# Gate and up projection of a SwiGLU layer as seven products of block sums (Strassen's scheme) in place of eight block products

## The chip, the cores and the metric

The kernel runs on 1 core of one Trainium2 chip, as one launch. The metric is the device time of one execution in microseconds (us). TensorE (PE) multiplies matrices into PSUM; VectorE (DVE), ScalarE (ACT) and GpSimd (POOL) work on elements; SyncE (SP) issues most of the DMAs. PEld is TensorE's loading of a stationary operand, which has an instruction of its own (LDWEIGHTS) ahead of each matmul.

## The reference

One residual layer on 512 tokens of width 1024, with 16 meta tokens ahead of them, all in float32: two kinds of attention, gates, an output projection, and then the part that this change is about, a SwiGLU feed-forward of width 2816 (22 blocks of 128):

```python
    merged = gates[:, :, 0] * y_sb + gates[:, :, 1] * y_df
    h = h + merged @ w_out[l]
    hn = rmsnorm(h, norm_ffn_g[l])
    h = h + (jax.nn.silu(hn @ w_ffn_gate[l]) * (hn @ w_ffn_up[l])) @ w_ffn_down[l]
y = rmsnorm(h, norm_final_g)
```

## The kernel before

**Precision.** Every float32 operand of a projection is split in two parts: `split` (L73 to L75) casts it to a rounded format on ScalarE (the high part, L74) and subtracts that on VectorE (the low part, L75). A product is then three matmuls, high by high, high by low and low by high (`mm3`, L142 to L147), which accumulate in one PSUM region. The stationary operand is a 128x128 block, the moving one has up to 512 columns.

**Weights.** All weight tiles stand in one list, `stream`, in the order of use; a tile is 128 partitions by 1024 numbers (512 KB). `stage` issues their DMAs on SP into `wst` (three buffers), up to 5 tiles ahead (STAGE); `weights` splits them into `wh` and `wl` (four buffers each), 2 ahead (READY). Apart from the start of the kernel, whose order is written out by hand, the compiler's planner sets the order on every engine when it compiles, from the order of the program, from priorities (`high_priority(offset=EVAC)` lifts a few instructions) and from its own cost estimates; at run time every engine goes through its list in order.

**Around the change.** `accumulate` (L776) computes `merged @ w_out` in two halves of 512 columns. As each group of 128 tokens is finished, `done` (L842) normalises it into `hn`; `turned(0)` and `turned(1)` (L827) transpose 256 tokens each on TensorE and evacuate them as `hT_h` (ScalarE, L838) and `hT_l` (VectorE, L839), with the 1024 channels on 8 blocks of partitions (`k`) and the tokens along the free axis. Block f = 0 of gate and up (`early`) is computed in two halves of 256 tokens, between the two calls of `turned`.

The loop at L865 then goes over f = 1 to 21. For each f it computes gate (L870) and up (L875): 8 blocks of `k`, three matmuls each, with 512 tokens as moving columns, so 48 matmuls per f. ScalarE applies SiLU (L872), VectorE multiplies (L876), and `split` makes `aT_h` and `aT_l` (L877), which the down projection (`accumulate` with the name "down", L898 and L899) reads as its stationary operand. Of the eight PSUM banks four belong to `ps_mm` (tag `mm`, also used for the transposes) and four to `ps_z` (two tiles of two banks).

Of the kernel before, what the change touches and what calls it, by code (L numbers as in the profile page):

```python
# [16 lines left out]
P = 128  # L17
D = 1024
# [21 lines left out]
def block_kernel(ctx: ExitStack, tc: tile.TileContext, x, meta, norm_mix_g, w_in, w_gate, b_gate,  # L40
# [72 lines left out]
    for half in range(2):  # L113
        for k0 in range(0, NFF, 2):
            rows(("down", half, k0), w_fd, half * 512, k0)

    staged, loaded = [], {}

    def stage(upto):
        for n in range(len(staged), min(len(stream), upto)):  # L120
            _, view, c0, cw, k0, k1 = stream[n]
            st = wpool.tile([P, k1 - k0, cw], F32, tag="wst", bufs=3, name="wst")
            staged.append(st)
            for a, b in ((0, 4), (4, 8)) if n < 2 else ((0, k1 - k0),):
                nc.sync.dma_start(st[:, a:b], view[:, k0 + a:k0 + b, c0:c0 + cw])

    def parts(n):
        k, _, _, cw, k0, k1 = stream[n]
        loaded[k] = tuple(wpool.tile([P, k1 - k0, cw], F32R, tag=t, name=t) for t in ("wh", "wl"))
        return loaded[k]  # L130

    def weights(key):
        at = next(i for i, c in enumerate(stream) if c[0] == key)
        if at < START:
            return loaded[key]
        stage(at + STAGE)
        for n in range(len(loaded), min(len(stream), at + READY)):
            wh, wl = parts(n)
            split(wh, wl, staged[n], nc.gpsimd if n < 3 else None)
        return loaded[key]  # L140

    def mm3(ps, pairs, start=True, stop=True):  # L142
        n = len(pairs)
        for i, (ah, al, bh, bl) in enumerate(pairs):
            nc.tensor.matmul(ps, lhsT=ah, rhs=bh, start=(start and i == 0), stop=False)  # L145
            nc.tensor.matmul(ps, lhsT=ah, rhs=bl, start=False, stop=False)  # L146
            nc.tensor.matmul(ps, lhsT=al, rhs=bh, start=False, stop=(stop and i == n - 1))  # L147

    def proj(ps, w, act, tok, ks=(0, KT)):
        (wh, wl), (ah, al) = w, act  # L150
# [624 lines left out]

    def accumulate(pool, name, act, nk, half, tail, done, banks, pieces=None):  # L776

        ah, al = act
# [7 lines left out]
        def step(k, t, c0, c1):  # L786
            wh, wl = weights((name, half, k // 2 * 2))
            q = slice(t * P, (t + 1) * P)
            mm3((acc[t] if c0 == 0 else extra)[:, c0:c1],
                [(ah[:, k, q], al[:, k, q], wh[:, k % 2, c0:c1], wl[:, k % 2, c0:c1])], k == 0, k == nk - 1)  # L790


        def cuts(t):
            return ((0, 256), (256, 512)) if t == NQ - 1 and pieces else ((0, 512),)

        for k in range(nk - tail):
            for t in range(NQ):
                for c0, c1 in cuts(t):
                    step(k, t, c0, c1)
        for t in range(NQ):  # L800
            for c0, c1 in cuts(t):
                for k in range(nk - tail, nk):
                    step(k, t, c0, c1)
                cs = slice(half * 512 + c0, half * 512 + c1)
                nc.vector.tensor_tensor(hres[:, t, cs], hres[:, t, cs], (acc[t] if c0 == 0 else extra)[:, c0:c1], op=ALU.add)
                sq = pool.tile([P, 512], F32, tag="sq", bufs=1, name="sq")
                s0, s1 = ssq[t][:, 0:1], ssq[t][:, 1:2]
                nc.scalar.activation(sq[:, c0:c1], hres[:, t, cs], AF.Square, accum_out=(s1 if half else s0))
# [11 lines left out]
    with tc.tile_pool(name="outp", bufs=1) as op_:  # L820
        hn = op_.tile([P, NQ, D], F32, name="hn")

        def normed(t):
            r = rstd(ssq[t][:, 1:2], more=ssq[t][:, 0:1])()
            nc.vector.tensor_scalar(hn[:, t], hres[:, t], r, None, op0=ALU.mult)

        def turned(tp):  # L827
            cs = slice(tp * 256, (tp + 1) * 256)
            for k in range(0, KT, 2):
                pt = tr_tile()  # L830
                for i in range(2):
                    for t in range(2):
                        nc.tensor.transpose(pt[:, (2 * i + t) * P:(2 * i + t + 1) * P],  # L833
                                            hn[:, 2 * tp + t, (k + i) * P:(k + i + 1) * P], ident)
                for i in range(2):
                    g = g_ffn[:, k + i:k + i + 1]
                    p = pt[:, i * 256:(i + 1) * 256]
                    nc.scalar.activation(hT_h[:, k + i, cs], p, AF.Copy, scale=g)  # L838
                    nc.vector.scalar_tensor_tensor(hT_l[:, k + i, cs], p, g, hT_h[:, k + i, cs].bitcast(F32),  # L839
                                                   op0=ALU.mult, op1=ALU.subtract)  # L840

        def done(t):  # L842
            normed(t)
            if t == 2:
                turned(0)

        accumulate(op_, "out", (mg_h, mg_l), KT, 0, 0, lambda t: None, "z")
        accumulate(op_, "out", (mg_h, mg_l), KT, 1, 6, done, "mm")

        early = [mm_tile(), mm_tile()]  # L850
        for ps, key in zip(early, (("fg", 0), ("fu", 0))):
            proj(ps[:, 0:256], weights(key), hT, slice(0, 256))
        turned(1)
        for ps, key in zip(early, (("fg", 0), ("fu", 0))):
            proj(ps[:, 256:512], weights(key), hT, slice(256, 512))
        use_table("silu_and_others")
    mid.close()


    with tc.tile_pool(name="ffn", bufs=1) as fp:  # L860
        aT_h = fp.tile([P, NFF, SEQ], F32R, name="aT_h")
        aT_l = fp.tile([P, NFF, SEQ], F32R, name="aT_l")
        gF = fp.tile([P, D], F32, name="gF")
        nc.gpsimd.dma_start(gF, norm_final_g.rearrange("(o d) -> o d", o=1).broadcast_to([P, D]))
        for f in range(NFF):  # L865
            if f == 0:
                pg, pu = early
            else:
                pg = mm_tile()
                proj(pg, weights(("fg", f)), hT, ALL)  # L870
            sg = fp.tile([P, SEQ], F32, tag="sg", bufs=2, name="sg")
            nc.scalar.activation(sg, pg, AF.Silu)  # L872
            if f:
                pu = mm_tile()
                proj(pu, weights(("fu", f)), hT, ALL)  # L875
            nc.vector.tensor_tensor(sg, pu, sg, op=ALU.mult)  # L876
            split(aT_h[:, f], aT_l[:, f], sg)  # L877
# [12 lines left out]

        def gained(t, cs):
            if len(outs) == t:
                outs.append(fp.tile([P, D], F32, tag="outs", name="outs", bufs=2))
# [4 lines left out]
        accumulate(fp, "down", (aT_h, aT_l), NFF, 0, 0, lambda t: None, "z")  # L898
        accumulate(fp, "down", (aT_h, aT_l), NFF, 1, 6, finish, "mm", gained)  # L899


# [27 lines left out]
```

## Time and profile before

| | |
|---|---|
| median of 3 runs | 1004.76 us (1004.44 to 1005.29) |
| profiled execution | 1004.22 us, its span 1002.5 us |
| granted TensorE clock | 0.996 of full speed, mean |
| TensorE matmul busy | 986.8 us, 5529 matmuls |
| weight loads busy | 855.2 us |
| VectorE / ScalarE / GpSimd busy | 526.5 / 451.0 / 109.9 us |
| gate and up, f = 1 to 21 | 645.69 to 874.19 us of the span |
| down projection | from 874.19 us |

The span is what the profile of one execution covers; 1.72 us of that execution's time lie around it. A timeline row gives start, duration, engine, line, operation, destination and source with shapes, and in brackets how long the engine had been idle and what ended that. A row of a group gives total busy time, the mean duration of one, and the idle time before its instructions with what ended it. Matmuls are pipelined: the duration of one is longer than the step from its start to the next one's.

### The profile page before, as it was taken

Reading aid. Unit: us, or ns where it says so; the run is one execution under the profiler, and the core shown is the slowest. Engines: PE = TensorE matmul, PEld = TensorE weight load, DVE = VectorE, ACT = ScalarE, POOL = GpSimd, SP = SyncE. Lnnn points to the kernel's source line nnn. Section 1 sums busy time; section 2 is a strip of 40 time slices with the busy share of each in tenths; the row PEclk is TensorE's granted clock in tenths of the full one; section 3 lists DMA queues with packets and bytes.
Section 4 is the critical chain, followed back from the end, with each engine's and each line's share of the span. In section 5 each row is a group of like instructions: output and inputs, shape, how many; then the busy total and the mean of one; then the engine's idle time right before and its main releaser. Section 6 shows DMA issues by size and latency. Waiting matters only on the chain.

```text
span 1002.5 us, 14077 instructions
## 1 busy us (share of the span) xinstructions
PE 986.8 (98%) x5529; PEld 855.2 (85%) x5529; DVE 526.5 (53%) x974; ACT 451.0 (45%) x848; POOL 109.9 (11%) x152
## 2 busy tenths in 40 slices
PE   7999999999999999999999999999999999999997
PEld 5999899998889999889878888888888888888886
DVE  7665446667777777777763334633333333312323
ACT  5655564555455666555653333623232232311313
POOL 4000000000122121122013220000000000000103
PEclk9999999999999999999999999999999999999998
DMA  6322222222333332333223352433333333232212
GB/s 198 106 64 63 85 85 63 85 64 64 86 105 86 106 85 65 105 85 86 84 84 85 104 177 76 122 91 103 99 91 105 87 103 103 87 105 88 102 42 85
DMA packets 129733, 93.01 MB, mean 93 GB/s; under 512 B 3681, under 2 KB 114434, under 8 KB 129666
## 3 DMA queue, kind: packets, MB, share of 16 engines
q1 hardware_dynamic: 127506, 85.09, 28.2%
q0 software_dynamic: 2000, 6.95, 2.6%
q8 instruction: 43, 0.70, 0.3%
q14 instruction: 24, 0.20, 0.1%
q10 hardware_dynamic: 160, 0.07, 0.0%
HBM read 85.67 MB, written 2.10 MB: 88 GB/s over the span
## 4 chain that ended last, share of the span: by engine, by line
PE 93%; DVE 3%; ACT 2%; issue 0%; DMA 0%; POOL 0%; SPq 0%; DVEq 0%; ACTq 0%; POOLq 0%
PE mm L145 25%; PE mm L146 24%; PE mm L147 24%; PE z L145 4%; PE z L146 4%; PE z L147 4%; PE tr L301 2%; PE z L432 1%; PE z L433 1%; PE tr L276 1%; PE z L325 0%; PE tr L313 0%; DMA xs<-in_x_dram 0%; PE tr L833 0%; DVE xs L608 0%
## 5 line engine op out<-in xcount | busy, mean ns | idle before, releaser
L75 DVE TENSOR_TENSOR wl<-wst,wh 128x1024 fp32r<-128x1024 f32 x150 | 185.8, 1239 | 256.8 <-ACT wh L74 254.3
L74 ACT CAST wh<-wst 128x1024 fp32r<-128x1024 f32 x150 | 157.9, 1052 | 358.7 <-PE mm L146 267.5
L145 PE MATMUL mm<-xT_h,wh 128*128 128x264 f32 (+2 forms) x776 | 249.1, 321 | 1.0 <-DVE dk L413 0.8
L146 PE MATMUL mm<-xT_l,wh 128*128 128x264 f32 (+2 forms) x776 | 246.9, 318 | 0.4 <-DVE xT_l L619 0.3
L147 PE MATMUL mm<-xT_h,wl 128*128 128x264 f32 (+2 forms) x776 | 246.1, 317 | 0.0
L145 PEld LDWEIGHTS mm<-xT_h,wh 128*128 128x128 f32 x776 | 146.1, 188 | 11.7 <-ACT xT_h L618 1.0
L146 PEld LDWEIGHTS mm<-xT_l,wh 128*128 128x128 f32 x776 | 146.0, 188 | 10.1 <-DVE xT_l L619 0.7
L147 PEld LDWEIGHTS mm<-xT_h,wl 128*128 128x128 f32 x776 | 146.0, 188 | 10.0
L146 PE MATMUL mm<-hT_l,wh 128*128 128x512 f32 (+1 forms) x368 | 139.9, 380 | 0.0
L145 PE MATMUL mm<-hT_h,wh 128*128 128x512 f32 (+1 forms) x368 | 139.7, 380 | 0.1
L147 PE MATMUL mm<-hT_h,wl 128*128 128x512 f32 (+1 forms) x368 | 139.7, 380 | 0.0
L145 PEld LDWEIGHTS mm<-hT_h,wh 128*128 128x128 f32 x368 | 69.0, 188 | 13.6 <-ACT hT_h L838 0.4
L146 PEld LDWEIGHTS mm<-hT_l,wh 128*128 128x128 f32 x368 | 69.2, 188 | 13.2 <-DVE hT_l L839 0.2
L147 PEld LDWEIGHTS mm<-hT_h,wl 128*128 128x128 f32 x368 | 69.2, 188 | 13.1
L145 PE MATMUL mm<-o_h,wh 128*128 128x512 f32 x128 | 53.2, 415 | 0.0
L876 DVE TENSOR_TENSOR sg<-mm,sg 128x512 f32<-128x512 f32 x22 | 15.2, 691 | 70.8 <-PE mm L147 70.8
L146 PE MATMUL mm<-o_l,wh 128*128 128x512 f32 x128 | 50.1, 391 | 0.8 <-DVE o_l L504 0.8
L147 PE MATMUL mm<-o_h,wl 128*128 128x512 f32 x128 | 50.1, 391 | 0.0
L282 POOL COPY v_s<-vT 128x16 f32<-128x16 f32 x64 | 21.8, 369 | 210.0 <-ACT vT L287 210.0
L460 ACT ACTIVATE pr<-pr,nm 128x144 f32<-128x144 f32 (+3 forms) x64 | 36.3, 568 | 14.2 <-DVE nm L458 14.1
L145 PE MATMUL z<-wh,aT_h 128*128 128x512 f32 (+1 forms) x110 | 40.5, 368 | 0.0
L146 PE MATMUL z<-wl,aT_h 128*128 128x512 f32 (+1 forms) x110 | 40.5, 368 | 0.0
(227 smaller groups left out, 1538.3 us busy)
## 6 DMA issues: line engine op xcount, KB each, us to landing
wst<-in_w_in_dram SPq DMA_DIRECT2D x46, 512.0 KB, 3.9
wst<-in_w_ffn_gate_dram SPq DMA_DIRECT2D x22, 512.0 KB, 3.8
wst<-in_w_ffn_up_dram SPq DMA_DIRECT2D x22, 512.0 KB, 3.8
wst<-in_w_ffn_down_dram SPq DMA_DIRECT2D x22, 512.0 KB, 3.6
wst<-in_w_gate_dram SPq DMA_DIRECT2D x16, 512.0 KB, 3.9
dk<-dk POOLq DMA_DIRECT2D x16, 264.0 KB, 4.9
wst<-in_w_br_sb_dram SPq DMA_DIRECT2D x8, 512.0 KB, 3.5
wst<-in_w_br_df_dram SPq DMA_DIRECT2D x8, 512.0 KB, 3.6
```

The source lines that it names most:

```text
L74: (hi_copy or nc.scalar.copy)(hi, src)
L75: (lo_eng or nc.vector).tensor_tensor(lo, src, hi.bitcast(F32), op=ALU.subtract)
L145: nc.tensor.matmul(ps, lhsT=ah, rhs=bh, start=(start and i == 0), stop=False)
L146: nc.tensor.matmul(ps, lhsT=ah, rhs=bl, start=False, stop=False)
L147: nc.tensor.matmul(ps, lhsT=al, rhs=bh, start=False, stop=(stop and i == n - 1))
L276: nc.tensor.transpose(pt[:, j * P:(j + 1) * P], vT[:, j * P:(j + 1) * P], ident)
L282: nc.gpsimd.tensor_copy(v_s[:, 32 * t:32 * t + NM], vT[:, (t + 1) * P:(t + 1) * P + NM])
L301: nc.tensor.transpose(pt[:, (t - j) * P:(t - j + 1) * P], blocks(t, j * P, (j + 1) * P), ident)
L432: nc.tensor.matmul(o, lhsT=q[c][:, qs], rhs=k[c][:, 0, k0:k1], start=True, stop=False)
L433: nc.tensor.matmul(o, lhsT=q[c][:, qs], rhs=k[c][:, 1, k0:k1], start=False, stop=True)
L460: nc.scalar.activation(pr[:, c], pr[:, c], AF.Exp, bias=nm[:, c:c + 1], accum_out=ls[:, t, c:c + 1])
L876: nc.vector.tensor_tensor(sg, pu, sg, op=ALU.mult)
```

## The change

For f = 1 to 21, gate and up are taken as a 2x2 matrix of blocks (gate and up, by the two halves K1 and K2 of the 1024 channels), and the activations as another (K1 and K2, by the token halves T1 and T2 of 256). Their product is formed from seven products of block sums (a form of Strassen's scheme with 15 block additions); each of the seven is 4 blocks of `k` by three matmuls of 256 columns, so 84 matmuls of 256 columns per f.

- Activation sums are formed once: ScalarE evacuates each transposed block a second time in full float32 (`bf`), `block_sums` makes the four sums and splits them into `t1` to `t4`.
- Weight sums are formed per f: jobs `c1` to `c4` add halves of the staged gate and up tiles on VectorE and split them into four `wh`/`wl` buffers.
- Each f has three PSUM tiles, `e1`, `e2`, `e3`. Two of the sums of products are left to PSUM accumulation, after the content so far has been copied out (`qx`, `qy`, `q1`); the rest are additions of 256 columns on VectorE.
- Products of two successive f are interleaved: `second(f)`, `first(f + 1)`, `third(f)`.
- `aT` is kept once in float32 and split as the down projection goes, for each of its two halves, in `act`.
- The up tiles have a staging buffer of their own, `wsu` (two buffers). The pools `tp`, `ffw` and `dw` are new, `outp` is gone; `hn` and `bf` lie in buffers of the pool `opool` that the attention used.

```diff
...
+    at_of = {c[0]: n for n, c in enumerate(stream)}
+    first_ffn = at_of["fg", 1]
     staged, loaded = [], {}
+    fpools = {}
...
+            key, view, c0, cw, k0, k1 = stream[n]
+            if key[0] == "fu" and key[1]:
+                if "w" not in fpools:
+                    return
+                st = fpools["w"].tile([P, KT, P], F32, tag="wsu", bufs=2, name="wsu")
+            else:
+                st = wpool.tile([P, k1 - k0, cw], F32, tag="wst", bufs=3, name="wst")
             staged.append(st)
...
+    tp = tp_ctx.enter_context(tc.tile_pool(name="tp", bufs=1, side="right"))
+    tsum = {n: tuple(tp.tile([P, 4, 256], F32R, name=f"{n}_{c}") for c in "hl") for n in ("t1", "t2", "t4")}
+    tsum["t3"] = tuple(v[:, K1, T2] for v in hT)
+    for n, k, t in (("b11", K1, T1), ("b21", K2, T1), ("b22", K2, T2)):
+        tsum[n] = tuple(v[:, k, t] for v in hT)
+    hn = opool.tile([P, NQ, D], F32, tag="y_df", name="hn", bufs=1)
+    bf = [[opool.tile([P, 4, 256], F32, tag=t, name="bf") for _ in range(2)] for t in ("o_h", "o_l")]
...
+                nc.scalar.activation(bf[k // 4][tp_][:, (k + i) % 4], p, AF.Copy, scale=g)
+    def block_sums():
+        (b11, b12), (b21, b22) = bf
+        sub, add = ALU.subtract, ALU.add
+        nc.vector.tensor_tensor(b11, b11, b12, op=sub)
+        nc.vector.tensor_tensor(b12, b22, b12, op=sub)
+        nc.vector.tensor_tensor(b22, b11, b22, op=add)
+        nc.vector.tensor_tensor(b21, b22, b21, op=sub)
+        th, tl = tsum["t2"]
+        nc.scalar.activation(th, b22, AF.Copy, scale=-1.0)
+        nc.vector.scalar_tensor_tensor(tl, b22, -1.0, th.bitcast(F32), op0=ALU.mult, op1=sub)
+        for n, v in (("t1", b11), ("t3", b12), ("t4", b21)):
+            split(*tsum[n], v)
...
+    block_sums()
+    use_table("silu_and_others")
...
     with tc.tile_pool(name="ffn", bufs=1) as fp:
-        aT_h = fp.tile([P, NFF, SEQ], F32R, name="aT_h")
-        aT_l = fp.tile([P, NFF, SEQ], F32R, name="aT_l")
+        aT = fp.tile([P, NFF, SEQ], F32, name="aT")
...
+        def c1(f):
+            wh, wl = chunk(1)
+            split(wh, wl, staged[at_of["fg", f]])
+            ops[f, "a11"], ops[f, "a12"] = (wh[:, K1], wl[:, K1]), (wh[:, K2], wl[:, K2])
+        def c2(f):
+            g, u = staged[at_of["fg", f]], staged[at_of["fu", f]]
+            s = fw.tile([P, KT, P], F32, tag="s21", bufs=2, name="s21")
+            nc.vector.tensor_tensor(s[:, K2], u[:, K1], u[:, K2], op=ALU.add)
+            nc.vector.tensor_tensor(s[:, K1], s[:, K2], g[:, K1], op=ALU.add)
+            wh, wl = chunk(2)
+            split(wh, wl, s)
+            ops[f, "s2"], ops[f, "s1"] = (wh[:, K1], wl[:, K1]), (wh[:, K2], wl[:, K2])
+            ops[f, "s"] = s
+        def c3(f):
+            g, u = staged[at_of["fg", f]], staged[at_of["fu", f]]
+            nc.vector.tensor_tensor(u[:, K1], g[:, K1], u[:, K1], op=ALU.add)
+            wh, wl = chunk(3)
+            split(wh, wl, u)
+            ops[f, "s3"], ops[f, "a22"] = (wh[:, K1], wl[:, K1]), (wh[:, K2], wl[:, K2])
+        def c4(f):
+            g, s = staged[at_of["fg", f]], ops[f, "s"]
+            nc.vector.tensor_tensor(g[:, K2], s[:, K1], g[:, K2], op=ALU.add)
+            wh, wl = chunk(4)
+            split(wh[:, K1], wl[:, K1], g[:, K2])
+            ops[f, "s4"] = wh[:, K1], wl[:, K1]
+        jobs = [(c1, 1), (c1, 2), (c2, 1), (c3, 1), (c4, 1)]
+        for f in range(2, NFF):
+            jobs += [(c2, f), (c3, f)] + [(c1, f + 1)] * (f + 1 < NFF) + [(c4, f)]
+        jobs += [(generic, n) for n in range(at_of["down", 0, 0], len(stream))]
...
+        def ready(upto):
+            for fn, f in jobs[made["n"]:upto]:
+                if fn is not generic:
+                    stage(at_of["fu", f] + 1)
+                else:
+                    stage(f + 3)
+                fn(f)
+                if fn is c4:
+                    stage(at_of["fu", f] + 6)
+            made["n"] = max(made["n"], upto)
...
+        def product(f, w, t, ps, start, stop):
+            (wh, wl), (th, tl) = ops[f, w], tsum[t]
+            mm3(ps, [(wh[:, k], wl[:, k], th[:, k], tl[:, k]) for k in range(4)], start, stop, True)
...
+        def first(f):
+            e1, e2, e3 = mm_tile()[:, 0:256], mm_tile()[:, 0:256], z_tile()[:, 0, 0:256]
+            sg = fw.tile([P, SEQ], F32, tag="sg", bufs=2, name="sg")
+            bank[f] = e1, e2, e3, sg
+            product(f, "a11", "b11", e1, True, True)
+            product(f, "a12", "b21", e2, True, True)
+            with tc.high_priority(offset=EVAC):
+                q1 = quarter("q1")
+                nc.scalar.copy(q1, e1)
+                nc.vector.tensor_tensor(sg[:, T1], e2, q1, op=ALU.add)
+            nc.scalar.activation(sg[:, T1], sg[:, T1], AF.Silu)
+        def second(f):
+            e1, e2, e3, sg = bank[f]
+            qx, qy = quarter("qx"), quarter("qy")
+            product(f, "s2", "t2", e1, False, True)
+            with tc.high_priority(offset=EVAC):
+                nc.scalar.copy(qx, e1)
+            ready(at_job(c3, f) + 2)
+            product(f, "s1", "t1", e3, True, True)
+            product(f, "s3", "t3", e1, False, True)
+            with tc.high_priority(offset=EVAC):
+                nc.scalar.copy(qy, e1)
+                nc.vector.tensor_tensor(qy, e3, qy, op=ALU.add)
+            return qx, qy
+        def third(f, qx, qy):
+            e1, e2, e3, sg = bank[f]
+            product(f, "a22", "t4", e1, False, True)
+            with tc.high_priority(offset=EVAC):
+                nc.vector.scalar_tensor_tensor(aT[:, f, T1], e1, -1.0, sg[:, T1], op0=ALU.mult, op1=ALU.mult)
+            product(f, "s4", "b22", e3, False, True)
+            with tc.high_priority(offset=EVAC):
+                nc.vector.tensor_tensor(sg[:, T2], e3, qx, op=ALU.add)
+            nc.scalar.activation(sg[:, T2], sg[:, T2], AF.Silu)
+            nc.vector.scalar_tensor_tensor(aT[:, f, T2], qy, -1.0, sg[:, T2], op0=ALU.mult, op1=ALU.mult)
+        sg = fw.tile([P, SEQ], F32, tag="sg", bufs=2, name="sg")
+        nc.scalar.activation(sg, early[0], AF.Silu)
+        nc.vector.tensor_tensor(aT[:, 0], early[1], sg, op=ALU.mult)
+        ready(3)
+        first(1)
+        ready(4)
+        first(2)
+        for f in range(1, NFF):
+            ready(at_job(c2, f) + 3)
+            rest = second(f)
+            if 1 < f < NFF - 1:
+                ready(at_job(c1, f + 1) + 2)
+                first(f + 1)
+            third(f, *rest)
+            ready(at_job(c4, f) + 2)
...
+        ffw_ctx.close()
+        tp_ctx.close()
+        dw_ctx = ExitStack()
+        dw = dw_ctx.enter_context(tc.tile_pool(name="dw", bufs=1, reuse_waits="tile"))
+        acts = []
+        def act(half, k):
+            m = half * NFF + k
+            for i in range(len(acts), min(2 * NFF, m + 3)):
+                a = dw.tile([P, 2, SEQ], F32R, tag="da", bufs=8, name="da")
+                split(a[:, 0], a[:, 1], aT[:, i % NFF])
+                acts.append(a)
+            return acts[m][:, 0], acts[m][:, 1]
+        def down_weights(key):
+            ready(jobs.index((generic, at_of[key])) + READY)
+            stage(at_of[key] + STAGE)
+            return loaded[key]
+        fpools["down"] = down_weights
...
```

More of the change, by code (lines that the diff above doesn't have):

```diff
@@ L819, in block_kernel @@
     hT = (hT_h, hT_l)
[L820 to L856, printed above, removed]
@@ new lines, in block_kernel, with normed, turned @@
+    bf = [[opool.tile([P, 4, 256], F32, tag=t, name="bf") for _ in range(2)] for t in ("o_h", "o_l")]
+    def normed(t):
+        r = rstd(ssq[t][:, 1:2], more=ssq[t][:, 0:1])()
+        nc.vector.tensor_scalar(hn[:, t], hres[:, t], r, None, op0=ALU.mult)
+    def turned(tp_):
+        cs = slice(tp_ * 256, (tp_ + 1) * 256)
+        for k in range(0, KT, 2):
+            pt = tr_tile()
+            for i in range(2):
+                for t in range(2):
+                    nc.tensor.transpose(pt[:, (2 * i + t) * P:(2 * i + t + 1) * P],
+                                        hn[:, 2 * tp_ + t, (k + i) * P:(k + i + 1) * P], ident)
+            for i in range(2):
+                g = g_ffn[:, k + i:k + i + 1]
+                p = pt[:, i * 256:(i + 1) * 256]
+                nc.scalar.activation(hT_h[:, k + i, cs], p, AF.Copy, scale=g)
+                nc.vector.scalar_tensor_tensor(hT_l[:, k + i, cs], p, g, hT_h[:, k + i, cs].bitcast(F32),
+                                               op0=ALU.mult, op1=ALU.subtract)
+                nc.scalar.activation(bf[k // 4][tp_][:, (k + i) % 4], p, AF.Copy, scale=g)
@@ new lines, in done, with merged @@
+    def done(t):
+        normed(t)
+        if t == 2:
+            turned(0)
+    def merged(half, k):
+        return mg_h[:, k], mg_l[:, k]
+    accumulate(mgp, "out", merged, KT, 0, 0, lambda t: None, "z")
+    accumulate(mgp, "out", merged, KT, 1, 6, done, "mm")
+    early = [mm_tile(), mm_tile()]
+    for ps, key in zip(early, (("fg", 0), ("fu", 0))):
+        proj(ps[:, 0:256], weights(key), hT, slice(0, 256))
+    turned(1)
+    for ps, key in zip(early, (("fg", 0), ("fu", 0))):
+        proj(ps[:, 256:512], weights(key), hT, slice(256, 512))
```

60 lines of the change are left out of this document (32 added, 28 removed).

## The prediction

> **What bounds the kernel now.** I read the page first, then the stage of gate and up by itself, then the steps of TensorE in it.
>
> ```profile
> PE 986.8 (98%) x5529; PEld 855.2 (85%) x5529; DVE 526.5 (53%) x974; ACT 451.0 (45%) x848; POOL 109.9 (11%) x152
> PEclk9999999999999999999999999999999999999998
> PE 93%; DVE 3%; ACT 2%; issue 0%; DMA 0%; POOL 0%; SPq 0%; DVEq 0%; ACTq 0%; POOLq 0%
> 645.69:874.19 228.50, 228.50 (x1010) 189.19 (x1009) 79.43 (x85) 66.95 (x85) 0.00 (x0) 1.00 0.34 99
> ```
>
> The first three lines are the page's: engines, granted clock, chain that ended last. The fourth is the view by windows: us, then busy time and count on PE, PEld, DVE, ACT and POOL, then clock, DMA share, GB/s. TensorE is the bound, at full clock; in the window of f = 1 to 21 it never rests, while VectorE is busy for 79.43 of 228.50 us and ScalarE for 66.95. Fewer TensorE columns are saved time one for one, until another engine is late.
>
> ```profile
> 645.69 0.40 PE L145 MATMUL mm<-hT_h,wh 128*128 128x512 f32 x1
> ...
> 874.19 0.39 PE L145 MATMUL z<-wh,aT_h 128*128 128x512 f32 x1
> 631.31 0.28 PE L145 MATMUL mm<-hT_h,wh 128*128 128x256 f32 x1
> ...
> 636.94 0.28 PE L147 MATMUL mm<-hT_h,wl 128*128 128x256 f32 x1
> 631.42 0.19 PEld L147 LDWEIGHTS mm<-hT_h,wl 128*128 128x128 f32 x1
> 631.54 0.19 PEld L145 LDWEIGHTS mm<-hT_h,wh 128*128 128x128 f32 x1
> ```
>
> The timeline gives the step of each shape. 512 columns: 1008 matmuls from 645.69 to 874.19, so 0.2267 us each and 10.88 us per f. 256 columns: 48 matmuls of block f = 0 start from 631.31 to 636.94, 47 steps of 0.1198 us. Each has its own weight load of 0.19 us, but the loads too start 0.12 us apart and run beside the matmul before: they cost nothing at this width.
>
> **The change, part by part.**
>
> TensorE in the loop: 84 x 0.1198 = 10.06 us per f in place of 10.88, so 0.82 us saved, 17.2 us over 21 f. That is the whole gain: one eighth of the columns less 5% that the shorter matmul loses per column.
>
> A rule of the Trainium skill speaks against it: page "TensorE: Matmul & The Clock Gate", Part 3, "The mechanism", says that a weight load overlaps a running matmul only where their row groups differ. All loads here use all rows, so by it load and matmul would stand one after the other (128/1.2 = 107 ns by the page's formula, an estimate, beside the 120 ns step); the rows at 631.42 and 631.54 show the overlap, so the trace does not agree.
>
> VectorE and ScalarE per f, with durations from the groups by shape:
>
> ```profile
> L75 DVE TENSOR_TENSOR wl<-wst,wh 128x1024 fp32r<-128x1024 f32 x150 | 185.8, 1239 | 256.8 <-ACT wh L74 254.3
> L75 DVE TENSOR_TENSOR aT_l<-sg,aT_h 128x512 fp32r<-128x512 f32 x22 | 15.0, 684 | 0.0
> L346 DVE TENSOR_TENSOR kl<-mm,kh 128x264 fp32r<-128x264 f32 x16 | 6.8, 425 | 0.2 <-ACT kh L345 0.2
> L839 DVE SCALAR_TENSOR_TENSOR hT_l<-tr,pcol,hT_h 128x256 fp32r<-128x256 f32 x16 | 7.5, 482 | 3.0 <-ACT hT_h L838 2.7
> L74 ACT CAST wh<-wst 128x1024 fp32r<-128x1024 f32 x150 | 157.9, 1052 | 358.7 <-PE mm L146 267.5 <-PE z L147 73.2 <-issue 10.9
> L74 ACT CAST aT_h<-sg 128x512 fp32r<-128x512 f32 x22 | 13.7, 622 | 0.5 <-DVE sg L876 0.5
> L287 ACT COPY vT<-mm 128x264 f32<-128x264 f32 x32 | 12.1, 378 | 16.5 <-PE mm L147 16.1
> ```
>
> VectorE: three low parts of 1024 (c1, c2, c3: 3 x 1.239), four sums of 512 and one low part of 512 (5 x 0.684), three additions of 256 (3 x 0.425), two multiplications of 256 (2 x 0.482): 3.72 + 3.42 + 1.28 + 0.96 = 9.38 us, against 79.43/21 = 3.78 before. ScalarE: 3 x 1.052 + 0.622 + five small ones at 0.378 = 5.67 us, against 3.19. So VectorE goes from a third of TensorE's period to 93% of it.
>
> ```profile
> 633.05 1.22 DVE L75 TENSOR_TENSOR wl<-wst,wh 128x1024 fp32r<-128x1024 f32 x1
> 634.19 0.21 DVE L225 TENSOR_SCALAR rs<-ssq 128x1 f32<-128x1 f32 x1
> 646.62 0.68 DVE L876 TENSOR_TENSOR sg<-mm,sg 128x512 f32<-128x512 f32 x1
> 647.22 1.22 DVE L75 TENSOR_TENSOR wl<-wst,wh 128x1024 fp32r<-128x1024 f32 x1
> ```
>
> Where the next VectorE instruction has its inputs, it starts 0.08 us before the end of the last (633.05 + 1.22 against 634.19; 646.62 + 0.68 against 647.22). Thirteen such overlaps make 9.38 into about 8.4 us. The Trainium skill, "VectorE: DVE Perf Modes", "The DRAIN you can't avoid", says that the next one does not start until the pipe is empty; by that it would stay 9.38, and the rows do not agree. Either way it is under 10.06, with 1.7 or 0.7 us of room.
>
> What can be late is a chain: sum on VectorE, cast on ScalarE, low part on VectorE. c2, c3 and c4 each have one, and where VectorE has nothing else ready it stands still for the cast (1.05, 1.05, 0.62 us). With four wh/wl buffers a chunk has some 4 to 7 us of TensorE work between the release of its buffer and its first product, so I take the chains as mostly hidden. The PSUM copies are shorter covers: `qx` is copied under s1.t1 (12 x 0.12 = 1.44 us) and can stand behind a cast of 1.05 on ScalarE; at f = 1 and f = 21 no `first` stands between `qy` and a22.t4, so its 0.38 is open. I take 2.5 us over the loop, between 0 and the rival below. The DMAs move the same bytes, issued by SP in list order; a `wsu` buffer is freed by c3(f) and needed by c2(f + 2), over 10 us later, where the window's share of 0.34 leaves room: nothing. POOL's queue gets nothing new.
>
> The start is dearer.
>
> ```profile
> 633.17 0.63 ACT L808 ACTIVATE sq<-hres 128x512 f32<-128x512 f32 x1 [0.55 <-DVE hres L805]
> 637.70 1.94 ACT L838 ACTIVATE hT_h<-tr,pcol 128x256 fp32r<-128x256 f32 x4 [3.24 <-PE tr L833]
> 640.53 2.06 ACT L838 ACTIVATE hT_h<-tr,pcol 128x256 fp32r<-128x256 f32 x4 [0.89 <-PE tr L833]
> 642.60 1.28 ACT L66 ACT_TABLE_LOAD   x1
> 636.08 0.75 DVE L825 TENSOR_SCALAR hn<-hres,rs 128x1024 f32<-128x1024 f32 x1
> 641.03 2.07 DVE L839 SCALAR_TENSOR_TENSOR hT_l<-tr,pcol,hT_h 128x256 fp32r<-128x256 f32 x4 [0.88 <-ACT hT_h L838]
> 645.57 0.28 PE L147 MATMUL mm<-hT_h,wl 128*128 128x256 f32 x1
> ```
>
> From 625 to 633 ScalarE is filled by turned(0) and casts. Eight more copies to `bf` (about 0.48 each, 0.39 apart: 3.1 us) push the square at 633.17 (the last tokens' norm, and all behind it to 637.70) by some 2 us. In turned(1) four evacuations for two blocks of `k`, at 0.45 each, take 1.8 us where the eight took 4.9 in all: 7.2, so 2.3 more. TensorE has 5.8 us of f = 0 to lay over it, but those need hT as well. I take 4 us of TensorE waiting before f = 1, bounds 1 and 6.
>
> Then `block_sums`, about 9 us of VectorE: three sums in a row behind the last `bf` (3 x 1.24), the low part of t2 (1.24) and three splits (3 x 1.15). The result of f = 0 on VectorE goes to `aT`, which takes the memory of the pool that holds `bf`, so it waits for all of them, and with it the PSUM bank of early[1] that first(2) wants. From the last `bf` TensorE has about 2 us of f = 0, 2.87 of first(1) and 1.44 of first(2), 6.3 in all, against 9 to 9.5: 3 us short. After that c3(1) (0.68 + 1.05 + 1.24) and the rest of c1, c2 stand in VectorE's queue ahead of s3.t3 with about the same length as TensorE's work: 0.5. Start together 7.5 us, bounds 3 (all in gaps) and 13 (nothing in gaps).
>
> The passage to the down projection:
>
> ```profile
> 873.97 0.39 PE L147 MATMUL mm<-hT_h,wl 128*128 128x512 f32 x1
> 874.46 0.69 DVE L876 TENSOR_TENSOR sg<-mm,sg 128x512 f32<-128x512 f32 x1 [3.38 <-PE mm L147]
> 976.00:992.90 16.90, 16.90 (x87) 14.44 (x86) 5.44 (x14) 4.88 (x13) 4.87 (x4) 1.00 0.13 49
> ```
>
> Before, the next matmul starts 0.22 us after the last of f = 21, on aT blocks long finished. Now its operand is split from `aT` into `da`, whose first buffer takes the memory of the loop's pool, by the order of allocation that of `sg`, last read by the last multiplication. So behind the last product stand an addition (0.43), SiLU (0.38), a multiplication (0.48), the cast (0.62) and hand-overs: 2.5 us, bounds 0 (another buffer lies there) and 3.5. In the down projection 44 splits add 0.62 to ScalarE and 0.68 to VectorE per 2.7 us of TensorE: covered. In the second half's last six blocks, where one is used every 0.68 us, 0.5 us (0 to 2), as VectorE has 5.44 of 16.90 there.
>
> Sum against the profiled execution of 1004.22 us (0.54 under the median of the runs, so I keep to it): -17.2 + 7.5 + 2.5 + 2.5 + 0.5 = -4.2, **1000.0 us**.
>
> **The rivals.**
>
> The chains show (ends slower): VectorE, in its fixed order, stands waiting for the casts of c2 and c3, so that the period of an f is 8.4 to 9.4 + 2.1, about 11.0 us, in place of 10.06. For it: three dependent pairs per f, and VectorE waited for ScalarE's cast 254.3 us before, at no cost then. Against it: other f's jobs can fill in. 21 x 0.94 = 19.7 instead of 2.5: 1017 us. It decides where the exposed waits exceed the room by 0.33 us per f (10.88 - 10.06 less 10.5/21 for start and passage).
>
> The start is hidden: gaps on VectorE and ScalarE (3.24 us before 637.70) take the copies and most sums, 3 us in place of 7.5, and passage and loop cost 1.5: 1004.2 - 17.2 + 4.5 = 991.5 us. For it: wh and wl for f = 1 and 2 can be made early. Against it: the three sums in a row need the last `bf`.
>
> The start is dearer, 12 us, with the rest as forecast: 1004.5 us, no change. For it: three engines hand over to each other there, each in fixed order.
>
> The change doesn't do what it says, as the weight loads show: at 0.188 us a load in place of 0.1198, 84 are 15.8 us per f, 4.9 more than now: 1107 us. Only the busy time of the loads speaks for it, the steps of 0.12 us against it.
>
> **How the numbers follow.** The forecast has 0.47, the hidden start 0.21, the chains 0.20, the dear start 0.10, the weight loads 0.02. About 0.2% (2 us) is what a measurement of this kernel can tell from no change: faster is below 1002.2. The forecast's own range, 995 to 1005, leaves three quarters of it there: 0.47 x 0.75 + 0.21 = 0.56 faster; same 0.11, from the forecast's upper end (0.07) and part of the dear start (0.04), since 2 us around 1004.2 hold it only in part; slower the rest, 0.33. The range goes from 990 (start 3, rest near 0) to 1015, most of the way to the chains' 1017.
>
> **What the profile after would show.** Right: steps of 0.12 us on TensorE throughout the loop; a period of 10.1 to 10.3 us per f from one a11.b11 to the next; VectorE busy nearly 90% of it; one or two gaps on TensorE between f = 0 and s3.t3 of f = 1, released by VectorE's t sums or by ScalarE's casts; one gap of 2 to 3 us ahead of the first down matmul, released by `da`. Wrong: a period above 10.4 with TensorE waiting for wl of c2 or c3 at every f; steps above 0.13 us; or a start without gaps.

## The result, and the profile after

The changed kernel takes 1010.35 us (median; 1009.99 to 1010.84) against 1004.81 (1004.44 to 1005.29) before: ratio 1.0055, 95% interval 1.0038 to 1.0073. It is slower by 0.4 to 0.7%; the forecast was 1000.0 and faster. The profiled execution took 1009.99 us, with a span of 1008.2 (before 1002.5).

First the page of the changed kernel: engines, granted clock, and the chain that ended last.

```profile
PE 974.9 (97%) x6285; PEld 880.4 (87%) x6285; DVE 659.9 (65%) x1214; ACT 544.7 (54%) x1026; POOL 109.7 (11%) x152
PEclk9999999999999999999999999999999999999997
ACT 0%; issue 0%
```

TensorE is busy for 11.9 us less than before, and the kernel is slower. The chain view, which named TensorE with 93% before, says nothing here: it starts at the last ScalarE instruction, for whose start the trace shows no releaser, and breaks off there. So I cut the span by TensorE's own marks and compared piece by piece. The view by windows of the changed kernel: the loop from s2.t2 of f = 1 to the last product, a stretch inside it, the gap ahead of the down projection, and what follows the last matmul.

```profile
656.44:865.73 209.29, 206.47 (x1718) 205.04 (x1716) 172.68 (x266) 115.81 (x188) 0.60 (x1) 1.00 0.37 109
700.00:850.00 150.00, 150.00 (x1259) 150.00 (x1258) 126.25 (x196) 82.76 (x135) 0.00 (x0) 1.00 0.35 103
865.73:869.85 4.12, 0.17 (x3) 0.00 (x1) 2.91 (x5) 3.42 (x5) 0.00 (x0) 0.97 0.42 146
992.21:1008.20 15.99, 0.28 (x3) 0.07 (x1) 3.97 (x14) 9.31 (x16) 3.97 (x4) 0.62 0.26 99
```

And the last of these windows in the kernel before, from its last matmul to the end of the span:

```profile
994.95:1002.50 7.55, 0.27 (x3) 0.07 (x1) 2.35 (x7) 1.73 (x5) 2.15 (x3) 0.64 0.37 140
```

The account, from the kernel before to the changed one:

| piece | how it is worked out | us |
|---|---|---|
| columns of gate and up | 1764 x 0.1198 = 211.3 in place of 228.5 | -17.2 |
| start | s2.t2 of f = 1 at 656.44; without waiting 645.69 + 48 x 0.1198 = 651.4 | +5.0 |
| loop | 209.29 less 1716 x 0.1198 = 205.6 | +3.7 |
| gap ahead of the down projection | 865.73 to 869.85 | +4.1 |
| down projection | 869.85 to 992.21 (122.4), before 874.19 to 994.95 (120.8) | +1.6 |
| after the last matmul | 16.0, before 7.55 | +8.4 |
| sum | spans: 1008.2 - 1002.5 = 5.7 | +5.6 |

TensorE finished at 992.21 in place of 994.95, 2.7 us earlier. All of the loss, and more, lies behind the last matmul: ScalarE is busy there for 9.31 us in 16 instructions instead of 1.73 in 5. Its timeline in the changed kernel, from a cast of a weight tile of the down projection and the SiLU of f = 20 on, then the last normalisation; the last row is VectorE's.

```profile
857.53 1.05 ACT L74 CAST wh<-wst 128x1024 fp32r<-128x1024 f32 x1 [0.82 <-PE z L160]
858.49 0.41 ACT L1009 ACTIVATE sg<-sg 128x256 f32<-128x256 f32 x1
858.92 1.28 ACT L66 ACT_TABLE_LOAD   x1
...
866.92 1.28 ACT L1009 ACT_TABLE_LOAD   x1
868.22 0.42 ACT L1009 ACTIVATE sg<-sg 128x256 f32<-128x256 f32 x1
869.18 3.22 ACT L74 CAST da<-aT 128x512 fp32r<-128x512 f32 x6 [0.55 <-DVE aT L1010]
...
999.38 1.28 ACT L238 ACT_TABLE_LOAD   x1
1000.68 0.30 ACT L238 ACTIVATE rs<-ssq 128x1 f32<-128x1 f32 x1
1000.99 1.28 ACT L240 ACT_TABLE_LOAD   x1
1002.29 0.20 ACT L240 ACTIVATE rs<-rs 128x1 f32<-128x1 f32 x1
1002.52 0.22 DVE L249 SCALAR_TENSOR_TENSOR rs<-rs 128x1 f32<-128x1 f32 x1 [2.91 <-ACT rs L240]
```

The same places in the kernel before:

```profile
875.19 0.62 ACT L74 CAST aT_h<-sg 128x512 fp32r<-128x512 f32 x1
875.83 1.28 ACT L66 ACT_TABLE_LOAD   x1
...
996.71 0.29 ACT L224 ACTIVATE rs<-ssq 128x1 f32<-128x1 f32 x1
997.03 0.20 ACT L226 ACTIVATE rs<-rs 128x1 f32<-128x1 f32 x1
```

A normalisation takes a logarithm (L238) and an exponential (L240). Before, one table for both was loaded at 875.83, after the last SiLU, and served all four normalisations. In the changed kernel that load stands at 858.92, ahead of the last SiLU. The SiLU then needs its own table back (866.92), and from there each normalisation loads one table for the logarithm and another for the exponential: 2.56 us more. Four of the 16 instructions behind the last matmul are such loads (5.1 us); the seven others that were not there before are the normalisation before the last and the first half of the last one's squares, pushed back into this window by the loads ahead of them.

Why there? `use_table` keeps its load behind the ScalarE instruction traced before it, and nothing else. In the kernel before that was the cast of the last `aT_h`, which comes after the last SiLU. In the changed kernel no such cast is left in the loop; what is traced last on ScalarE is the cast of a down-projection weight tile out of `ready`, which is ready early. The planner put it (857.53), and the load behind it (858.92), ahead of the last SiLU.

### The profile page after: what moved, and what is told of

Same layout as the page of the kernel before. It is cut to its first block, busy times and chain, and to the rows that moved or that the text cites. A ratio compares the mean times of both kernels' runs of the same rounds, so it can differ in the third digit from the quotient of the medians.

```text
span 1008.2 us, 16022 instructions
## 1 busy us (share of the span) xinstructions
PE 974.9 (97%) x6285; PEld 880.4 (87%) x6285; DVE 659.9 (65%) x1214; ACT 544.7 (54%) x1026; POOL 109.7 (11%) x152
## 5 line engine op out<-in xcount | busy, mean ns | idle before, releaser
L75 DVE TENSOR_TENSOR wl<-wst,wh 128x1024 fp32r<-128x1024 f32 (+1 forms) x150 | 174.3, 1162 | 150.2 <-ACT wh L74 149.8
L74 ACT CAST wh<-wst 128x1024 fp32r<-128x1024 f32 (+1 forms) x150 | 148.6, 992 | 172.4 <-PE mm L160 112.0
L159 PE MATMUL mm<-hT_h,wh 128*128 128x256 f32 x284 | 80.6, 286 | 1.8 <-ACT hT_h L860 0.9
L160 PE MATMUL mm<-hT_l,wh 128*128 128x256 f32 x284 | 81.1, 286 | 1.0 <-DVE hT_l L861 1.0
L161 PE MATMUL mm<-hT_h,wl 128*128 128x256 f32 x284 | 81.0, 286 | 0.2 <-DVE wl L75 0.2
L159 PEld LDWEIGHTS mm<-hT_h,wh 128*128 128x128 f32 x284 | 53.9, 191 | 2.7 <-ACT hT_h L860 1.4
L159 PE MATMUL mm<-t_h,wh 128*128 128x256 f32 x168 | 47.4, 282 | 0.5 <-ACT qy L997 0.5
L160 PE MATMUL mm<-t_l,wh 128*128 128x256 f32 x168 | 47.2, 281 | 0.0
L161 PE MATMUL mm<-t_h,wl 128*128 128x256 f32 x168 | 47.2, 282 | 0.0
L159 PE MATMUL z<-wh,da 128*128 128x512 f32 (+1 forms) x110 | 41.3, 376 | 4.0 <-ACT da L74 4.0
```

The lines of the kernel that those rows point to most:

```text
L74: (hi_copy or nc.scalar.copy)(hi, src)
L75: (lo_eng or nc.vector).tensor_tensor(lo, src, hi.bitcast(F32), op=ALU.subtract)
```

## The experiments

Each gives the median beside that of the kernel before on the same chip. "s2.t2" is the time at which TensorE starts s2.t2 of f = 1.

**The table load alone, taken back.**

```diff
         nc.scalar.activation(sg[:, T2], sg[:, T2], AF.Silu)
+        if f == NFF - 1:
+            use_table(LN_EXP)
...
-        use_table(LN_EXP)
```

> The changed kernel with one line moved: the load of ScalarE's table for logarithm and exponential is written right behind the last SiLU of f = 21, so that the planner has to keep it there. Theory (tables): in the changed kernel this load stands ahead of the last SiLU; SiLU then loads its own table again (1.28 us, in the passage), and in the end each of the four norms loads a table for Ln and one for Exp (2.56 us each). Without that the time from the last matmul to the end of the span goes from 15.8 to about 7.4 us, the gap ahead of the first down matmul from 4.0 to 2.7, and the median from 1010.35 to about 1000.6 us. Rival (the end waits for the new memory of the down projection, or its splits): the loads lie beside other work, the end stays over 12 us long, and the time stays at 1008 or more.

Measured: 1000.57 us (1000.3 to 1001.27) against 1004.59, ratio 0.9963 [0.9948, 0.9977]. One moved line is worth 9.8 us by the medians and turns the change into a gain. Between the two profiled executions it is 8.7 us: 7.4 behind the last matmul, 0.4 at the passage, 0.3 at the start and 1.6 in the loop (207.7 us from s2.t2 to its end, for 209.3), less 1.0 by which the down projection is longer (123.4 for 122.4). The loop's 1.6 us are not shown to come from the line: TensorE's longest wait there, at f = 2, has to do with a DMA (below). The window behind the last matmul, still 1.0 us longer than in the kernel before, and the passage to the down projection:

```profile
990.93:999.50 8.57, 0.28 (x3) 0.07 (x1) 2.88 (x8) 1.73 (x5) 2.03 (x3) 0.79 0.33 123
```

```profile
865.15 0.42 ACT L1009 ACTIVATE sg<-sg 128x256 f32<-128x256 f32 x1 [0.20 <-DVE sg L1008]
865.58 1.28 ACT L66 ACT_TABLE_LOAD   x1
866.88 3.22 ACT L74 CAST da<-aT 128x512 fp32r<-128x512 f32 x6
867.54 0.79 PE L159 MATMUL z<-wh,da 128*128 128x512 f32 x1 [3.60 <-ACT da L74]
```

ScalarE is back to 1.73 us in 5 instructions behind the last matmul. But the load now stands between the last SiLU and the first `da` cast, and TensorE waits for that cast: 3.60 us, where 2.7 were expected.

**The same load put ahead of the last SiLU in the kernel before.** If its place alone costs that much, it must cost it without Strassen too.

```diff
+            if f == NFF - 1:
+                use_table(LN_EXP)
             nc.scalar.activation(sg, gt, AF.Silu)
...
-        use_table(LN_EXP)
```

> The kernel before the change, with the same load written ahead of the last SiLU instead of behind the loop; nothing else. Tables: the same loads appear in the end, and the kernel goes from 1004.8 to about 1013 us, with some 15 us from the last matmul to the end instead of 7.4; the extra load ahead of SiLU is hidden, as TensorE has other work there. Rival (the end was long for another reason): at most the last norm's two loads show, 1004.8 to 1007.5 us.

Measured: 1012.3 us (1011.72 to 1012.99) against 1004.59, ratio 1.008 [1.0064, 1.0097]. Behind its last matmul:

```profile
994.46:1010.00 15.54, 0.28 (x3) 0.07 (x1) 3.97 (x14) 9.31 (x16) 3.97 (x4) 0.63 0.27 102
```

The same 9.31 us in the same 16 ScalarE instructions. Both directions are shown: of the 8.4 us lost behind the last matmul, e1 takes back 7.4 and e2 adds 8.0 without a product changed.

**The passage: memory or queue?** With e1's edit, and a tile of 4 KB a partition ahead of the first `da`, so that `da` does not lie on `sg`:

```diff
+        dw.tile([P, 1024], F32, name="pad_sg")
         acts = []
```

> As e1_pin, and one unused tile of 4 KB per partition is allocated first in the pool of the down projection, so that the first da buffer no longer lies on the memory of sg, which the last multiplication of f = 21 reads. Theory (memory): what is left of the gap ahead of the first down matmul, 2.7 us, is the chain last product, addition, SiLU, multiplication, cast into that memory; with another place the cast runs earlier, the gap is under 0.6 us, the slow matmuls after it (1.3 us) go too, and the time is 996.5 to 997.5 us. Rival (order): ScalarE and VectorE get to the splits no earlier, as their queues are full to the end of the loop; the gap stays near 2.7 and the time at 1000.6 us.

Measured: 1001.78 us (998.24 to 1002.21) against 1004.59, ratio 0.9964 [0.9953, 0.9975]. The gap is still 3.60, released by `da`. The memory theory falls: in e1 the cast starts 0.02 us behind the table load and waits for nothing else (866.88), and in the changed kernel only the last 0.55 us ahead of the first `da` cast is a wait for the last multiplication (row 869.18). The cast is late because it stands on ScalarE behind the last SiLU and the table load.

**The loop's waits.** With e1's edit, `wsu` with three buffers in place of two:

> As e1_pin, with three staging buffers for the up tiles instead of two; the order of TensorE's instructions is the same. Theory (DMA): the two waits of TensorE in the first rounds of the loop (1.3 us ahead of s4.b22 of f = 2 at 684.6, 0.7 at 689.8) come from VectorE standing still for an up tile (2.7 and 1.7 us) and then doing a 1.2 us instruction ahead of an evacuation; with a third buffer both go, and the time is 998.2 to 998.8 us. Rival (backlog): VectorE is behind from the start of the loop anyway, the waits only move: 1000.6 us.

Measured: 1000.75 us (999.47 to 1001.51) against 1004.59, ratio 0.9962 [0.9947, 0.9977]. No gain over e1. TensorE's waits of over half a us in the loop, in the changed kernel:

```profile
684.59 0.39 PE L159 MATMUL z<-hT_h,wh 128*128 128x256 f32 x1 [1.30 <-DVE qy L998]
689.82 0.38 PE L159 MATMUL mm<-hT_h,wh 128*128 128x256 f32 x1 [0.68 <-ACT qx L992]
```

The first of them goes back to an up tile that came late from DRAM: VectorE waited for it ahead of a sum, and the evacuation `qy` stood behind that.

```profile
682.38 0.69 DVE L925 TENSOR_TENSOR s<-wsu 128x512 f32<-128x512 f32 x1 [1.72 <-DMA wsu<-in_w_ffn_up_dram]
```

With three buffers both are gone (206.5 us from s2.t2 to the end of the loop, 207.7 in e1), and VectorE no longer waits for an up tile there (17 waits, 11.1 us, in e1; for gate tiles it now waits 4.7). But in e1, with two buffers, the first of TensorE's waits is absent too and the second is 0.51 us, so the moment at which a tile landed in one execution has a part in it. And s2.t2 starts at 657.81 instead of 656.11: a sum on VectorE ahead of an `hT_l` waited 0.97 us for its `wsu` tile (0.50 in e1), TensorE waited 1.16 us for that `hT_l` (0.69 in e1), and behind this wait the clock was half where it is full in e1. The window from 643 to 646 in e1, with 27 matmuls, and in this run, with 15:

```profile
643.00:646.00 3.00, 3.00 (x27) 2.92 (x26) 3.00 (x6) 2.06 (x5) 0.00 (x0) 1.00 0.02 5
643.00:646.00 3.00, 2.98 (x15) 2.98 (x15) 3.00 (x5) 1.49 (x4) 0.00 (x0) 0.51 0.02 5
```

What the loop won, the start lost, and most of that loss is the clock.

**The start.** TensorE's waits there in the changed kernel, and the granted clock in a window behind them:

```profile
638.75 0.87 PE L855 MATMUL tr<-ident,hn 128*128 128x128 f32 x6 [0.86 <-DVE hn L847]
...
640.90 0.58 PE L160 MATMUL mm<-hT_l,wh 128*128 128x256 f32 x1 [0.54 <-DVE hT_l L861]
647.68 0.50 PE L159 MATMUL mm<-hT_h,wh 128*128 128x256 f32 x2 [0.70 <-ACT hT_h L860]
648.66 0.39 PE L160 MATMUL mm<-hT_l,wh 128*128 128x256 f32 x1 [0.47 <-DVE hT_l L861]
```

```profile
641.00:644.00 3.00, 3.00 (x14) 2.98 (x15) 3.00 (x7) 2.29 (x6) 0.00 (x0) 0.50 0.00 0
```

TensorE waits for transposed blocks, not for the activation sums; the clock behind these gaps is half. In e1, with nearly the same waits (0.87, 0.24 and 0.69 us), it stays at 1.00 (line above), and from the first of them to s2.t2 it is 17.1 us instead of 17.7: the half clock is worth some 0.5 us here. Three experiments, each with e1's edit, ask who is late: ScalarE with its `bf` copies, or VectorE with the weight sums that stand between the `hT_l`.

ScalarE's copies cut to 32 of 256 columns; the other columns of `bf` are left out and stay zero:

> As e1_pin, but the second evacuation of the transposed blocks copies only 32 of the 256 columns into bf (the rest of bf is set to zero before by GpSimd, so the block sums are of other numbers). Theory (ScalarE): the 5 us that TensorE reaches the first product of t2 later than the columns account for come from ScalarE's 16 extra evacuations: shortened from 0.47 to about 0.2 us each they give back 2.5 to 4 us, 997 to 998 us. Rival (VectorE): the low parts of hT stand behind additions of weight halves and block sums in VectorE's queue; then at most 1 us comes back, 999.5 to 1000.6 us.

Measured: 997.73 us in one run, against 1004.76 (no interval); s2.t2 at 654.16 instead of 656.11, or 1.7 us earlier if both are counted from the first transposition of `turned(1)` (637.50 here, 637.72 in e1). The copies cost something under 2 us of the start. One execution can't say it closer: e3, whose start is that of e1, has s2.t2 at 655.10.

The copies moved to GpSimd, as an addition:

```diff
-   nc.scalar.activation(bf[...], p, AF.Copy, scale=g)
+   nc.gpsimd.tensor_tensor(bf[...], hT_h[...], hT_l[...], op=ALU.add)
```

> As e1_pin, with bf formed on GpSimd as the sum of hT_h and hT_l in place of the second evacuation on ScalarE; the result is the same sum. ScalarE theory: 16 evacuations fewer on ScalarE, the start gets 2 to 4 us shorter, 996.6 to 998.6 us, unless GpSimd (16 additions of 256 columns, some 0.7 us each) becomes the last to deliver bf. VectorE theory: no gain, and as GpSimd and VectorE work at once the start gets longer, 1000.6 to 1004 us.

Measured: 1003.84 us (1002.23 to 1005.06) against 1004.76, ratio 0.9989 [0.998, 0.9999]; s2.t2 at 658.21. It is some 3 us slower than e1. GpSimd and VectorE in this kernel:

```profile
641.39 3.69 POOL L863 TENSOR_TENSOR bf<-hT_h,hT_l 128x256 f32<-128x256 f32 x4 [6.68 <-DVE hT_l L861]
646.82 1.89 POOL L863 TENSOR_TENSOR bf<-hT_h,hT_l 128x256 f32<-128x256 f32 x2 [1.74 <-DVE hT_l L861]
```

```profile
640.23 0.69 DVE L926 TENSOR_TENSOR s<-wsu 128x512 f32<-128x512 f32 x1 [1.88 <-DMA wsu<-in_w_ffn_up_dram]
641.62 1.06 DVE L927 TENSOR_TENSOR s<-s,wst 128x512 f32<-128x512 f32 x1
643.39 1.11 DVE L935 TENSOR_TENSOR wsu<-wst,wsu 128x512 f32<-128x512 f32 x1
645.12 1.23 DVE L869 TENSOR_TENSOR bf<-bf 128x1024 f32<-128x1024 f32 x1 [0.62 <-POOL bf L863]
648.03 1.76 DVE L75 TENSOR_TENSOR t_l<-bf,t_h 128x1024 fp32r<-128x1024 f32 x1
```

An addition of 512 columns takes VectorE 0.69 us where GpSimd is idle, and 1.06 and 1.11 while GpSimd adds; one of 1024 takes 1.23 and 1.76. Work given to GpSimd came back as longer instructions on VectorE. TensorE waited 1.35 and 1.50 us for `hT_l` there, and the clock was 0.50 from 643.5 to 646.5, so the longer instructions are not all of the loss.

VectorE's part: everything of f = 1 and 2 queued on it behind the last `hT_l`.

```diff
+        with tc.issue_after(last_lo[0].ins):    # the last hT_l
             ready(3)
             first(1)
             ready(4)
             first(2)
```

> As e1_pin, with VectorE's weight sums and splits for f = 1 and 2 queued behind the last low part of hT, nothing else. VectorE theory: an addition of up halves waits for its DMA ahead of the low parts of hT and holds them up; without it the T2 half of block f = 0 is done 1.5 to 3 us earlier, 998 to 999.5 us, unless the sums are then late for s2.t2. ScalarE theory: no gain at that place, and the sums are later: 1000.6 to 1003 us.

Measured: 1004.95 us (1002.1 to 1005.65) against 1004.76, ratio 0.9998 [0.9989, 1.0008], some 4 us slower than e1. The transposed blocks did come earlier: TensorE was through with all that lies ahead of s2.t2 at 654.3, 1.8 us sooner than in e1. Then it stood for a cast of ScalarE, which waited for the weight sums of VectorE. The wait, the first of the two sums, and the window behind the wait:

```profile
658.48 0.39 PE L159 MATMUL mm<-t_h,wh 128*128 128x256 f32 x1 [3.98 <-ACT wh L74]
```

```profile
654.93 0.69 DVE L927 TENSOR_TENSOR s<-wsu 128x512 f32<-128x512 f32 x1
```

```profile
658.48:664.72 6.24, 5.38 (x25) 5.18 (x26) 6.21 (x10) 3.54 (x6) 0.00 (x0) 0.56 0.52 169
```

The first weight sum now starts at 654.93, and behind that gap the clock is 0.56 for 6 us. Early sums delay the blocks and late ones the first products.

**The passage closed.** From the changed kernel: one `da` block split four f earlier into a buffer of its own, the table load behind the tenth split of the down projection, the 4 KB tile, and three `wsu` buffers.

```diff
+            if f == NFF - 4:
+                early_acts(1)    # split(da_early, aT[:, 0])
...
+                if i == 9:       # in act(), where the splits are traced
+                    use_table(LN_EXP)
```

> As e6_wsu3 (third up buffer), with three edits at the passage to the down projection: the first da block is split four f earlier into a buffer of its own, the unused 4 KB tile keeps the other da buffers off sg, and the table for logarithm and exponential is loaded behind the tenth split instead of ahead of the first. Theory (queue): the gap of 3.6 us ahead of the first down matmul was ScalarE's queue: last SiLU, table load of 1.28 us, cast of 0.62; TensorE now has 2.7 us of work on the early block over it, the gap falls under 1 us, the 1.5 us at half clock go, and the time is 995.5 to 997 us. Rival (PSUM): the first down matmuls wait for the last evacuation of a z bank instead; then 1.5 to 2 us of the gap stay, 998 to 999.5 us.

Measured: 995.0 us (994.6 to 995.08) against 1004.76, ratio 0.9902 [0.9888, 0.9917]: the best version. TensorE and ScalarE at the passage:

```profile
860.27 0.40 PE L159 MATMUL z<-wh,da_early 128*128 128x512 f32 x1
...
865.24 0.50 PE L159 MATMUL z<-wh,da_early 128*128 128x512 f32 x1 [0.54 <-DVE sg L1016]
```

```profile
871.41 1.28 ACT L66 ACT_TABLE_LOAD   x1
```

The planner laid the first down matmuls among the last products; one wait of 0.54 is left of 3.6 to 4, and the clock stays at 1.00 there. The edits were measured together; the tile (e3) and the third buffer (e6) alone brought nothing over e1.

**A finer hold at the start.** The version before, with only c3(1), c4(1), c2(2) and first(2) queued behind the last `hT_l`:

> The kernel of e8_passage (995.0), with the sums of c3(1), c4(1) and c2(2) and the evacuations of first(2) queued on VectorE behind the last hT_l; c1 and the sums of c2(1) stay where they were, ahead of it. In e9_start everything was held back: TensorE came to the end of f = 0 and first(1), first(2) about 2 us earlier, and then stood 4.1 us for the cast of c2(1). Theory (the small additions between the hT_l delay the transposed blocks, and only c2(1) is needed early): TensorE comes to s2.t2 of f = 1 about 1 to 1.5 us earlier (656 in place of 657.1) and no new wait of over 0.5 us follows: 993.5 to 994.3. Rival (VectorE has no room there at all: what is held back is late by as much as it was early): a wait of 1 us or more for wh or wl of c3(1) or c4(1) behind s2.t2, 995 to 997.

Measured: 995.46 us (994.5 to 995.76) against 1004.57, ratio 0.9911 [0.9894, 0.9927]: not to be told from 995.0. s2.t2 starts at 655.03 instead of 657.13, but a wait of 0.53 for a `wh` follows, which with the slower steps behind it takes 1.2 us (a wait of 0.46 for `qy` has its like in the version before, 0.44), and in the profiled executions 0.6 us of the 2.1 are left. The theory's 656 held, its price did not.

Nor do the 2.1 us belong to the hold alone. The same window of the start, in the version before and in this one:

```profile
643.00:646.00 3.00, 3.00 (x16) 3.00 (x16) 2.45 (x4) 0.95 (x2) 0.00 (x0) 0.50 0.03 5
643.00:646.00 3.00, 2.88 (x24) 2.64 (x22) 2.44 (x4) 2.66 (x6) 0.00 (x0) 1.00 0.02 5
```

From TensorE's wait for an `hT_l` to its next wait for an `hT_h` it was 7.4 us in the version before (640.96 to 648.38), 5.7 here, and 6.0 in e1 (641.28 to 647.25), which holds nothing back and has the full clock. So most of the 2.1 us is the clock; whether the hold kept it up is not shown. Whether another order keeps the 2 us was not tried.

## Why the prediction was wrong, by its steps

- **TensorE's columns: right.** 1259 matmuls in 150.00 us are 0.119 us each, 10.01 us per f, with weight loads for each beside them. The rival of the weight loads is out.
- **VectorE and ScalarE per f: right.** 126.25 of 150 us are 8.4 us per f on VectorE, the value with the overlaps; ScalarE has 5.5 (forecast 5.67). VectorE is 84% busy, not "nearly 90%". The chains are hidden: TensorE loses 3.7 us over the whole loop (forecast 2.5), in waits for `qy` and `qx`, which the step had named as short covers, and in smaller ones. The longest, 1.30 us for `qy`, has a cause that the step had put at nothing, an up tile that came late (row 682.38). VectorE waited for up tiles 18 times in the loop, 11.2 us in all, mostly at no cost. The slower rival, 19.7 us there, did not happen, though the time did come out slower.
- **The start: 5.0 for 7.5, within its bounds, for other reasons in part.** The copies to `bf` cost something under 2 us (e4). The 3 us charged to `block_sums` did not appear as a wait for t sums; the step's own items (4 x 1.24 and 3 x 1.15) add up to 8.4 us, not 9 to 9.5, which would have made it 2.1. TensorE waited for `hT_l` and `hT_h`, and a stretch at half clock added some 0.5 us.
- **The passage: the size was too small, the reason was mostly another.** 4.1 us for 2.5 and its bound of 3.5. The chain of addition, SiLU, multiplication and cast was right; the memory of `sg` was not its cause (e3), and a table load of 1.28 us was in it. Behind it the clock fell, so the down projection cost 1.6 us; the 0.5 forecast for it were for waits in its last blocks, and TensorE has none in that window.
- **The step that failed: the list of what moves.** The prediction said that the new code casts `aT` in another place, but did not follow what had stood behind that cast. The load of the table, one line that the change leaves as it was, hung on it. So the sum had no term behind the last matmul, where 8.4 us were lost; up to there the pieces come to -2.8 us, where the forecast's terms come to -4.2. The kernel before shows the row that it would have taken: 875.83, a table load just behind the `aT_h` cast, and no load in the normalisations at the end. With the load back in place, e1 took 1000.57 us, but the nearness to 1000.0 is in part luck, errors of opposite sign: the start was charged too much, the loop, the passage and the down projection too little.

The bracketed waits of the trace do not name it: VectorE waits 2.91 us for `rs`, nobody for the table. What tells it is the list of ScalarE's instructions in a window, against that of the kernel before.

The halved clock at the passage, in the view by windows of the changed kernel and of e1:

```profile
869.85:873.00 3.15, 3.15 (x7) 2.44 (x8) 3.15 (x6) 3.15 (x7) 0.00 (x0) 0.50 0.45 163
866.50:872.50 6.00, 4.96 (x12) 3.89 (x13) 4.99 (x9) 4.62 (x9) 0.00 (x0) 0.50 0.49 163
```

The Trainium skill, "TensorE: Matmul & The Clock Gate", Part 1, says that at least one window of about 3.4 us without work halves the clock and at least one of about 3.4 us of work restores it. Here a gap of 4.12 us was followed by 0.50 up to 873, and the 0.54 us of the version with the passage closed by no fall, which agrees. In e1 it fits less well: its loop's last matmul ends at 863.94, the clock is already 0.50 at 866.50, 2.6 us later, and it stays there up to 872.50, through 5.0 us of work. The longer stretch at half clock is where e1's down projection loses its 1.0 us. That the clock was at 0.50 in 641 to 644 of the changed kernel too, behind several waits of 0.5 to 0.9 us with short bursts between them, this sentence of the page does not cover; nor does the trace explain it, as e1 has nearly the same waits at 1.00.

## What to carry to other kernels

A change that removes or moves an instruction also moves whatever is ordered only behind it: look for order that hangs on "the instruction before", table loads above all, and follow it to the end of the kernel. Cut the span by the bottleneck engine's own first and last instruction of each stage; if that engine ends earlier and the kernel later, the loss is behind it, and the counts of each engine in that window name it. When fewer columns are bought with more work on other engines, the steady loop can come out as computed, and the bill lies at its two ends.

## What the runs showed of the hardware

- A table load took 1.28 us in every row shown, and the next activation starts 0.02 us behind it (999.38 + 1.28, then 1000.68). The Trainium skill, "ScalarE: Activation LUTs", "What ACT_TABLE_LOAD costs", gives 1283 ns for the load and adds a drain of about 1380; the load agrees, no drain shows in these rows.
- Logarithm and exponential share one table if it is the one loaded; once another has been loaded, each of the two brought a table of its own, at every normalisation: eight loads at the end of the changed kernel, none in the kernel before.
- VectorE's additions with two inputs become 1.4 to 1.6 times as long while GpSimd adds (0.69 to 1.06 and 1.11 us; 1.23 to 1.76 us, where GpSimd adds during a part of it).
